# A two-layer decoder trunk: transposes in the gate's PSUM banks, a plain first gate, up before gate, and 64 bytes between tiles

## The chip, the cores and the metric

The kernel runs on one core of one Trainium2 chip. The metric is the time of one execution on the device in microseconds. An engine executes its own instructions in order and waits on semaphores for those of the others: TensorE (PE; its weight loads are listed as PEld), VectorE (DVE), ScalarE (ACT), and SyncE (SP), which issues the DMAs.

## The reference

The input is x, 256 tokens of width 2048 in float32. There are two layers, each with four attention groups behind one input projection, and a gated feed-forward part of 5632 hidden columns. What the change touches is the feed-forward part:

```
for l in range(DEPTH):                       # DEPTH = 2
    x = x + hybrid_mixer(rms_norm(x, attn_norm[l]), w_in[l], ..., w_out[l], ...)
    h = rms_norm(x, ffn_norm[l])
    x = x + (silu(h @ w_gate[l]) * (h @ w_up[l])) @ w_down[l]
return rms_norm(x, final_norm)
```

## The kernel before

x lies transposed in SBUF, in eight tiles X of 128 partitions x 2 x 256. Products are made in float32r with both factors split in a rounded part and a rest: XS holds the two parts of x times the norm's gain, and each weight becomes wh (ACT, L241) and wl (DVE, L242). A product of two split factors is three matmuls: high by high, low by high, high by low. The norm's factor itself (r_x, made by `rsq`) is applied behind the projections; `rcol` turns it by a small matmul (L424) into rxc, one number per token.

The weights come in units of 2048 columns, 1 MB each, in the order in which `pack_weights` wrote them; `fetch` gives each a raw buffer of three and one DMA on SP. wh and wl have six buffers each of 1024 columns. Three ways of multiplying matter here. `Acc.wide` and `Acc.narrow` have the weight standing still and 256 or 512 columns of x or h moving. `ProjV.step` has x standing still and 512 columns of the weight moving, 24 matmuls per unit; `up` and the v projections use it. `ProjSW.step`, the gate, does a Strassen step on blocks: seven products instead of eight, so 2 x 21 matmuls of 256 columns per unit, for which DVE builds sums of weight blocks (L348 to L353) and splits them (L354, L356), and sums of x blocks, xs_sum, are built once per layer (L762 to L777). `ProjSW.out` (L373) adds the seven products up again.

The feed-forward part runs over 11 groups of 512 hidden columns. In a group, `gate_up` takes four steps of the gate and four of `up`, in turns (in group 0 all of `up` first), makes silu(gate) times up (L796, L798), and `turn` transposes this tile `hid` with eight small matmuls (L807) and splits it into two tiles h. From group 2 on, each group is followed by four products of the down projection (`down`, eight after the last group), each of 16 pairs of a 512-column and a 256-column matmul, which `add_to` (L283, L284) adds to X. An even group turns its tile after its first down product. An odd group's tile is turned inside the next group's `gate_up`.

PSUM is divided into two tiles of two banks (accp: one for `up`, each down product and the transposes) and four of one bank (attp: the gate's seven products, and small ones). The order of the instructions on each engine is set when the program is built: the tile framework takes the program's order, lays it on a simulated timeline and issues what is ready there first. Tiles are given out pool by pool in the order of L189 to L197; the four one-line gaps of 8 floats (32 bytes) at L204 shift the pools' places within 128 bytes. In before, counted in bytes past a multiple of 128, raw lies at 0, XS, wh and wl at 32, h at 64, xs_sum at 96.

Of the kernel before, what the change touches and what calls it, by code (L numbers as in the profile page):

```python
# [8 lines left out]
F32 = mybir.dt.float32  # L9
F32R = mybir.dt.float32r  # L10
AF = mybir.ActivationFunctionType
OP = mybir.AluOpType
# [14 lines left out]
LINE = 8  # L27
RAW_B, W_B, H_B, Q_B4, T2, SG = 3, 6, 7, 8, 3, 3
NG = HID // 512

Q_LAT, KV_LAT, K_ROPE = 0, 512, 1024
Q_B, K_B, V_B = 1088, 1600, 2112
# [83 lines left out]
def pack_weights(w_in, w_uq, w_ukv, w_out, w_gate, w_up, w_down):  # L116
    us = []
    for l in range(DEPTH):
        m = w_in[l]
        us += quad_units(m, Q_LAT) + quad_units(m, KV_LAT)  # L120
        misc = np.zeros((D, 128), np.float32)
        misc[:, :64] = m[:, K_ROPE:K_ROPE + 64]
        misc[:, 64:68] = m[:, F_C:F_C + 4]
        us.append(unit(misc, 0, 16, 0, 128))

        def qkv(q0, k0, v0):
            r = []
            for c0 in (q0, q0 + 256, k0, k0 + 256):
                r += pair_units(m, c0)
            return r + quad_units(m, v0)  # L130

        us += qkv(Q_B, K_B, V_B)
        uq = w_uq[l].reshape(512, 4, 192)
        us.append(unit(uq[:, :, 128:].reshape(512, 256), 0, 4, 0, 256))
        us.append(unit(uq[:, :, :128].reshape(512, 512), 0, 4, 0, 512))
        ukv = w_ukv[l].reshape(512, 4, 256)
        us.append(unit(ukv[:, :, :128].reshape(512, 512), 0, 4, 0, 512))
        us.append(unit(ukv[:, :, 128:].reshape(512, 512), 0, 4, 0, 512))
        us += qkv(Q_C, K_C, V_C)
        us += qkv(Q_D, K_D, V_D)  # L140
        m = w_out[l]
        for c0 in range(0, D, 256):
            us.append(unit(m, 0, 6, c0, 256))
            us.append(unit(m, 6, 6, c0, 256))
        for c0 in range(0, D, 512):
            us.append(unit(m, 12, 4, c0, 512))

        def gate(g, i):
            return quarters(w_gate[l], 4 * i, 512 * g)

        def up(g, i):
            return unit(w_up[l], 4 * i, 4, 512 * g, 512)

        def dn(k0, n, ps):
            cols = 2048 // n
            return [unit(w_down[l], k0, n, c0 * cols, cols) for c0 in ps]

        for g in range(NG):
            if g == 0:
                us += [up(g, i) for i in range(4)] + [gate(g, i) for i in range(4)]  # L160
            else:
                for i in range(4):
                    us += [gate(g, i), up(g, i)]
            for c, ps in down_after(g):
                us += dn(8 * c, 8, ps)
        us += dn(8 * (NG // 2), 4, range(4))
    return np.concatenate([u.reshape(-1) for u in us])
# [17 lines left out]
def trunk(ctx: ExitStack, tc: tile.TileContext, x_d, w_d, sm_d, c_d, out_d):  # L185
# [15 lines left out]
    A.preload_act_table_set(LNEXP)  # L201

    X = [cp.tile([128, 2, S], F32, name=f"X{i}") for i in range(8)]
    for p in (cp, gp0, gp, gp1):  # L204
        p.tile([128, LINE], F32, name="gap")
    XS = [cp.tile([128, 2, 2, S], F32R, name=f"XS{i}") for i in range(8)]
    sm = cp.tile([128, SM_N], F32, name="sm")
    cst = cp.tile([128, C_N], F32, name="cst")
# [123 lines left out]

    class ProjSW:
        def __init__(self, sums):
            self.sums = sums
            ps = [attp.tile([128, 2, S], F32, name="att") for _ in range(4)]
            self.p = {1: ps[0][:, 0], 2: ps[0][:, 1], 3: ps[1][:, 0], 6: ps[2][:, 0],
                      7: ps[2][:, 1], 5: ps[3][:, 0], 4: ps[3][:, 1]}

        def step(self, k0):  # L340
            raw = fetch()
            for j in range(2):
                i = k0 // 2 + j
# [29 lines left out]
        def out(self):  # L373
            p = self.p
            c = [tp.tile([128, 512], F32, name="ff_g", tag="t2", bufs=T2) for _ in range(2)]
            c11, c12, c21, c22 = c[0][:, :256], c[0][:, 256:], c[1][:, :256], c[1][:, 256:]
            A.activation(c11, p[1], AF.Copy)
            V.tensor_add(c12, c11, p[6])
            V.tensor_add(c11, c11, p[2])
            V.tensor_add(c21, c12, p[7])  # L380
            V.tensor_sub(c12, c12, p[5])
            V.tensor_sub(c22, c21, p[5])
            V.tensor_add(c21, c21, p[4])
            V.tensor_add(c12, c12, p[3])
            return c

    def sumsq(srcs):
# [11 lines left out]
    def rsq(tot, n, name, more=None):  # L399
# [10 lines left out]
        a, ln = tot[:, 1, :], tot[:, 0, :]  # L410
        V.tensor_scalar(a, ps[:, :S], 1.0 / n, EPS, op0=OP.mult, op1=OP.add)
        A.activation(ln, a, AF.Ln)
        r0 = tp.tile([128, S], F32, name="rq_r", tag="t2", bufs=T2)
        A.activation(r0, ln, AF.Exp, scale=-0.5)
        V.tensor_mul(ln, r0, r0)
        V.scalar_tensor_tensor(a, ln, -0.5, a, op0=OP.mult, op1=OP.mult)
# [147 lines left out]
    for l in range(DEPTH):  # L564
# [190 lines left out]
        last_out(grp[3], sb + SM_FFN)  # L755
        rf = rsq(sumsq(X), D, "r_x")

        rfc = rcol(rf, "rxc")
        rfn = tp.tile([128, 2], F32, name="rfn", bufs=1)
        V.tensor_scalar(rfn, rfc, -1.0, None, op0=OP.mult)  # L760

        sums = []  # L762
        for i in range(8):
            xg = tp.tile([128, 2, S], F32, name="xg", tag="sg", bufs=SG)
# [13 lines left out]

        last_act = [None]

        def gate_up(g, turn_last):
            up = ProjV(xk, KT)
            if g == 0:
                for i in range(4):
                    up.step(4 * i)
            gate = ProjSW(sums)
            for i in range(4):
                gate.step(4 * i)
                if g > 0:
                    up.step(4 * i)  # L790
                if i == 0 and turn_last is not None:
                    turn_last()
            hid = gate.out()
            for t in range(2):
                for col, r in ((slice(0, 256), rfc), (slice(256, 512), rfn)):
                    last_act[0] = A.activation(hid[t][:, col], hid[t][:, col], AF.Silu,  # L796
                                               scale=r[:, t:t + 1])
                V.scalar_tensor_tensor(hid[t], up.out[t], rfc[:, t:t + 1], hid[t],  # L798
                                       op0=OP.mult, op1=OP.mult)
            return hid  # L800

        def turn(hid):
            pt = accp.tile([128, 2, 2, S], F32, name="acc")
            hs = [hp.tile([128, 2, 2, S], F32R, name="h") for _ in range(2)]
            for f in range(4):
                for t in range(2):
                    P.transpose(pt[:, f // 2, f % 2, t * 128:t * 128 + 128],  # L807
                                hid[t][:, f * 128:f * 128 + 128], ident)
            for p in range(2):
                split(hs[p], pt[:, p])  # L810
            hts.extend(hs)

        hts = []
# [3 lines left out]

        held = None
        for g in range(NG):
            hid = gate_up(g, None if held is None else (lambda v=held: turn(v)))  # L820
            held = hid
            if g == NG - 1:
                with tc.issue_after(last_act[0].ins):
                    A.preload_act_table_set(LNEXP)
            for n, (c, p) in enumerate((c, p) for c, ps in down_after(g) for p in ps):
                down(c, p)
                if n == 0 and g % 2 == 0:
                    turn(hid)
                    held = None
        nxt = (l + 1) * SM_L + SM_ATT if l + 1 < DEPTH else None  # L830
        last_out(lambda k: hts[4 * (NG // 2) + k // 2][:, k % 2], nxt)
# [46 lines left out]
```

## Time and profile before

| | us |
|---|---|
| median of 3 runs (2367.01 to 2367.73) | 2367.07 |
| the profiled execution, whole | 2368.98 |
| its span, first to last instruction | 2367.2 |
| PE busy in the span | 2268.4 |
| DVE busy | 1872.5 |
| ACT busy | 1271.2 |

A busy time is the time in which at least one instruction of the engine was running. Matmuls overlap, so a matmul's own duration (0.28 us for 256 columns) is not the pace at which they follow each other; the pace is read from the starts in a timeline, or from a row of the chain that merges many of them.

### The profile page before, as it was taken

The page shows a single profiled execution, that of the slowest core. Times are in us where ns is not written, and L with a number is a line of the kernel's source. Part 1 is how long each engine was busy: PE and PEld are TensorE (multiplying, and loading weights), DVE is VectorE, ACT ScalarE, POOL GpSimd, SP SyncE. Part 2 cuts the span into 40 slices and gives each one's busy share as a digit, 9 for nine tenths or more (in the row PEclk, how much of TensorE's full clock was granted, in tenths as well). Part 3 has the DMA queues.
Part 4 walks back from the last instruction along what each step waited for, and adds up shares of the span by engine and source line. Part 5 has one row for each costly group of instructions (what it writes and reads, how often), then busy time and mean ns, then how long its engine had stood idle before and what let it go on. Part 6 is the DMA issues. An engine that isn't in the chain of part 4 may idle for free.

```text
span 2367.2 us, 34828 instructions
## 1 busy us (share of the span) xinstructions
PE 2268.4 (96%) x13822; PEld 2028.1 (86%) x13822; DVE 1872.5 (79%) x2717; ACT 1271.2 (54%) x1653; POOL 0.2 (0%) x4
## 2 busy tenths in 40 slices
PE   8999999899999999999999999997999999999997
PEld 8888889688888888888998887896888888898887
DVE  7876667988887888788777765689988788797875
ACT  7454455654555545456555644656555455454554
POOL 0000000000000000000000000000000000000000
PEclk9999999999999999999999999999999999999999
DMA  7444446355554545455555344462555555454552
GB/s 290 175 155 175 141 147 212 109 179 195 196 199 177 178 177 196 163 211 196 185 189 183 129 160 143 138 218 107 196 192 182 195 196 196 161 186 170 205 205 89
DMA packets 61650, 419.90 MB, mean 177 GB/s; under 512 B 6832, under 2 KB 7088, under 8 KB 14768
## 3 DMA queue, kind: packets, MB, share of 16 engines
q1 hardware_dynamic: 61344, 417.63, 49.2%
q8 instruction: 108, 1.77, 0.3%
q14 instruction: 54, 0.44, 0.1%
q10 hardware_dynamic: 144, 0.07, 0.0%
HBM read 415.57 MB, written 2.10 MB: 176 GB/s over the span
## 4 chain that ended last, share of the span: by engine, by line
PE 90%; DVE 6%; ACT 2%; issue 1%; DMA 0%; DVEq 0%; ACTq 0%; SPq 0%
PE acc L258 67%; PE att L369 6%; PE att L370 6%; PE att L371 5%; PE att L258 4%; DVE wl L242 1%; DVE w_sum L348 1%; ACT wh L241 1%; PE acc L807 0%; PE att L492 0%; DVE w_sum L351 0%; DVE ff_g L798 0%; DVE w_sum L353 0%; PE att L501 0%; DVE wl L356 0%
## 5 line engine op out<-in xcount | busy, mean ns | idle before, releaser
L241 ACT ACTIVATE wh<-raw 128x1024 fp32r<-128x1024 f32 (+1 forms) x634 | 647.9, 1029 | 663.6 <-PE acc L258 601.9
L242 DVE TENSOR_TENSOR wl<-raw,wh 128x1024 fp32r<-128x1024 f32 (+1 forms) x634 | 744.5, 1181 | 284.2 <-ACT wh L241 282.3
L258 PE MATMUL acc<-h,wh 128*128 128x512 f32 (+1 forms) x1824 | 626.7, 389 | 32.5 <-DVE X L284 31.7
L258 PE MATMUL acc<-wh,XS 128*128 128x512 f32 x1792 | 576.4, 395 | 0.5 <-ACT wh L241 0.5
L258 PE MATMUL acc<-h,wl 128*128 128x256 f32 x1744 | 499.0, 286 | 0.0
L258 PEld LDWEIGHTS acc<-h,wh 128*128 128x128 f32 x1824 | 345.3, 192 | 103.0 <-issue 31.9
L258 PE MATMUL acc<-XS,wh 128*128 128x512 f32 (+1 forms) x1344 | 385.2, 352 | 19.6 <-DVE hilo L279 11.3
L258 PEld LDWEIGHTS acc<-wh,XS 128*128 128x128 f32 x1792 | 337.4, 188 | 75.1 <-ACT wh L241 0.7
L258 PE MATMUL acc<-wl,XS 128*128 128x512 f32 x896 | 353.6, 395 | 0.0
L258 PEld LDWEIGHTS acc<-h,wl 128*128 128x128 f32 x1744 | 337.4, 193 | 1.0
L258 PE MATMUL acc<-XS,wl 128*128 128x256 f32 x1056 | 303.0, 287 | 0.0
L258 PEld LDWEIGHTS acc<-XS,wh 128*128 128x128 f32 x1344 | 237.4, 192 | 53.2 <-DVE hilo L279 11.9
L355 ACT ACTIVATE wh<-w_sum 128x1024 fp32r<-128x1024 f32 x176 | 186.5, 1060 | 175.2 <-PE acc L258 72.3
L356 DVE TENSOR_TENSOR wl<-w_sum,wh 128x1024 fp32r<-128x1024 f32 x176 | 215.1, 1222 | 25.6 <-ACT wh L355 19.1
L354 DVE TENSOR_TENSOR wl<-raw,wh 128x768 fp32r<-128x768 f32 x176 | 167.6, 952 | 47.4 <-ACT wh L352 47.3
L258 PEld LDWEIGHTS acc<-XS,wl 128*128 128x128 f32 x1056 | 202.2, 192 | 0.8
L352 ACT ACTIVATE wh<-raw 128x768 fp32r<-128x768 f32 x176 | 148.5, 843 | 97.9 <-PE acc L258 94.8
L370 PE MATMUL att<-wh,xs_sum 128*128 128x256 f32 x704 | 197.1, 283 | 3.0 <-DVE xs_sum L776 3.0
L258 PEld LDWEIGHTS acc<-wl,XS 128*128 128x128 f32 x896 | 168.9, 188 | 35.5
L369 PE MATMUL att<-wh,xs_sum 128*128 128x256 f32 x704 | 194.6, 282 | 2.2 <-ACT xs_sum L775 1.6
L371 PE MATMUL att<-wl,xs_sum 128*128 128x256 f32 x704 | 193.9, 281 | 0.7 <-DVE wl L356 0.7
L369 PE MATMUL att<-wh,XS 128*128 128x256 f32 x528 | 150.7, 285 | 6.9 <-ACT wh L352 4.5
(187 smaller groups left out, 2758.7 us busy)
## 6 DMA issues: line engine op xcount, KB each, us to landing
raw<-in_w_dram SPq DMA_DIRECT2D x364, 1024.0 KB, 4.8
raw<-in_w_dram SPq DMA_DIRECT2D x32, 768.0 KB, 4.3
raw<-in_w_dram SPq DMA_DIRECT2D x8, 512.0 KB, 7.3
X<-in_x_dram SPq DMA_DIRECT2D x8, 256.0 KB, 6.6
out_dram<-X SPq DMA_DIRECT2D x8, 256.0 KB, 2.4
cst<-in_const_dram SPq DMA_DIRECT2D x1, 1216.0 KB, 8.7
raw<-in_w_dram SPq DMA_DIRECT2D x4, 256.0 KB, 4.8
cst<-in_const_dram SPq DMA_DIRECT2D x1, 67.0 KB, 7.4
```

Of the source, the lines that this page charges most:

```text
L241: A.activation(wh[:, i:e], raw[:, o + i:o + e], AF.Copy)
L242: V.tensor_sub(wl[:, i:e], raw[:, o + i:o + e], wh[:, i:e].bitcast(F32))
L258: P.matmul(out, lhsT, rhs, start=bank not in self.started, stop=stop, skip_group_check=True)
L348: V.tensor_add(t[:, :512].rearrange("p (a b) -> p a b", a=2), q[:, :512].rearrange("p (a b) -> p a b", a=2), q[:, 768:][:, None, :].to_bro ...
L352: A.activation(hs[:, :768], q[:, :768], AF.Copy)
L354: V.tensor_sub(ls[:, :768], q[:, :768], hs[:, :768].bitcast(F32))
L355: A.activation(ht, t, AF.Copy)
L356: V.tensor_sub(lt, t, ht.bitcast(F32))
L369: P.matmul(p, xh, wh[:, c], start=first, stop=False, skip_group_check=True)
L370: P.matmul(p, xl, wh[:, c], start=False, stop=False, skip_group_check=True)
L371: P.matmul(p, xh, wl[:, c], start=False, stop=i == 7, skip_group_check=True)
```

## The change

The transposes of `turn` take two one-bank tiles of attp, each with its own split behind it, instead of one accp tile. `ProjSW` takes its four attp tiles at its first step and not when it is made. In every group an `up` step stands ahead of the gate's step. Group 0's gate is a `ProjV` with plain weights, as wide as the Strassen one; its Silu covers 512 columns at once, and `rcol` with rxc and rfn moves behind its steps. An odd group with down products turns its tile after the last of them. In `ProjSW.out` the add of p[3] comes two operations earlier. `rsq` keeps r0 in a buffer of its own. The gap ahead of wh and wl grows from 32 to 96 bytes, which moves wh and wl to 96, h to 0 and xs_sum to 32 past a multiple of 128, while XS and raw stay.

```diff
+GAP_X, GAP_W, GAP_H, GAP_Q = 1, 3, 1, 1
...
         for g in range(NG):
-            if g == 0:
-                us += [up(g, i) for i in range(4)] + [gate(g, i) for i in range(4)]
-            else:
-                for i in range(4):
-                    us += [gate(g, i), up(g, i)]
+            for i in range(4):
+                us += [up(g, i), unit(w_gate[l], 4 * i, 4, 0, 512) if g == 0 else gate(g, i)]
...
-    for p in (cp, gp0, gp, gp1):
-        p.tile([128, LINE], F32, name="gap")
+    for p, n in ((cp, GAP_X), (gp0, GAP_W), (gp, GAP_H), (gp1, GAP_Q)):
+        p.tile([128, n * LINE], F32, name="gap")
...
             V.tensor_sub(c12, c12, p[5])
+            V.tensor_add(c12, c12, p[3])
             V.tensor_sub(c22, c21, p[5])
             V.tensor_add(c21, c21, p[4])
-            V.tensor_add(c12, c12, p[3])
...
-        r0 = tp.tile([128, S], F32, name="rq_r", tag="t2", bufs=T2)
+        r0 = tp.tile([128, S], F32, name="rq_r", bufs=1)
...
-        rfc = rcol(rf, "rxc")
-        rfn = tp.tile([128, 2], F32, name="rfn", bufs=1)
-        V.tensor_scalar(rfn, rfc, -1.0, None, op0=OP.mult)
...
         def gate_up(g, turn_last):
             up = ProjV(xk, KT)
-            if g == 0:
-                for i in range(4):
-                    up.step(4 * i)
-            gate = ProjSW(sums)
+            gate = ProjV(xk, KT) if g == 0 else ProjSW(sums)
             for i in range(4):
-                gate.step(4 * i)
-                if g > 0:
-                    up.step(4 * i)
+                up.step(4 * i)
                 if i == 0 and turn_last is not None:
                     turn_last()
-            hid = gate.out()
+                gate.step(4 * i)
+            if g == 0:
+                rc.append(rcol(rf, "rxc"))
+                rc.append(tp.tile([128, 2], F32, name="rfn", bufs=1))
+                V.tensor_scalar(rc[1], rc[0], -1.0, None, op0=OP.mult)
+                hid = [tp.tile([128, 512], F32, name="ff_g", tag="t2", bufs=T2) for _ in range(2)]
+            else:
+                hid = gate.out()
             for t in range(2):
-                for col, r in ((slice(0, 256), rfc), (slice(256, 512), rfn)):
-                    last_act[0] = A.activation(hid[t][:, col], hid[t][:, col], AF.Silu,
-                                               scale=r[:, t:t + 1])
-                V.scalar_tensor_tensor(hid[t], up.out[t], rfc[:, t:t + 1], hid[t],
+                if g == 0:
+                    A.activation(hid[t], gate.out[t], AF.Silu, scale=rc[0][:, t:t + 1])
+                else:
+                    for h in range(2):
+                        o = hid[t][:, h * 256:h * 256 + 256]
+                        last_act[0] = A.activation(o, o, AF.Silu, scale=rc[h][:, t:t + 1])
+                V.scalar_tensor_tensor(hid[t], up.out[t], rc[0][:, t:t + 1], hid[t],
                                        op0=OP.mult, op1=OP.mult)
...
         def turn(hid):
-            pt = accp.tile([128, 2, 2, S], F32, name="acc")
             hs = [hp.tile([128, 2, 2, S], F32R, name="h") for _ in range(2)]
-            for f in range(4):
-                for t in range(2):
-                    P.transpose(pt[:, f // 2, f % 2, t * 128:t * 128 + 128],
-                                hid[t][:, f * 128:f * 128 + 128], ident)
             for p in range(2):
-                split(hs[p], pt[:, p])
+                pt = attp.tile([128, 2, S], F32, name="att")
+                for f in range(2):
+                    for t in range(2):
+                        P.transpose(pt[:, f, t * 128:t * 128 + 128],
+                                    hid[t][:, (2 * p + f) * 128:(2 * p + f + 1) * 128], ident)
+                split(hs[p], pt)
...
-            hid = gate_up(g, None if held is None else (lambda v=held: turn(v)))
-            held = hid
+            hid = gate_up(g, held)
+            held = lambda v=hid: turn(v)
...
-            for n, (c, p) in enumerate((c, p) for c, ps in down_after(g) for p in ps):
+            todo = [(c, p) for c, ps in down_after(g) for p in ps]
+            for n, (c, p) in enumerate(todo):
                 down(c, p)
-                if n == 0 and g % 2 == 0:
-                    turn(hid)
+                if n == (0 if g % 2 == 0 else len(todo) - 1):
+                    held()
                     held = None
```

## Rows read from the trace of the kernel before

**Rows 1.** The page: busy time of PE, share of the span, instructions.
```profile
PE 2268.4 (96%) x13822; PEld 2028.1 (86%) x13822; DVE 1872.5 (79%) x2717; ACT 1271.2 (54%) x1653; POOL 0.2 (0%) x4
```
**Rows 2.** The waits of PE: us in total, times, longest.
```profile
PE acc L258 <- DVE X L284: 31.7, 10, 4.2
PE att L424 <- DVE r_x L418: 12.7, 2, 7.3
```
**Rows 3.** Timeline of PE (start, us, what), transposes of group 4.
```profile
840.90 1.04 PE L807 MATMUL acc<-cst,ff_g 128*128 128x128 f32 x8
845.98 0.76 PE L258 MATMUL acc<-h,wh 128*128 128x512 f32 x1 [4.05 <-DVE X L284]
...
846.76 0.63 PE L258 MATMUL acc<-h,wh 128*128 128x512 f32 x1
...
847.40 0.63 PE L258 MATMUL acc<-h,wh 128*128 128x512 f32 x1
```
**Rows 4.** Timeline of DVE in the same stretch.
```profile
845.16 0.68 DVE L284 TENSOR_TENSOR X<-X,acc 128x512 f32<-128x512 f32 x1
```
**Rows 5.** Windows: us, busy time of each engine (instructions), granted clock, DMA.
```profile
846.00:851.00 5.00, 5.00 (x15) 4.25 (x16) 0.43 (x1) 0.00 (x0) 0.00 (x0) 0.50 0.43 180
...
841.90:978.40 136.50, 132.45 (x801) 118.21 (x800) 112.68 (x151) 69.27 (x79) 0.00 (x0) 0.97 0.52 185
```
**Rows 6.** The chain that ended last (start, us, what): two steps of `up`.
```profile
597.52 5.58 PE acc L258 x24
607.98 5.58 PE acc L258 x24
```
**Rows 7.** Timeline of PE and DVE behind the gate of group 4.
```profile
829.64 0.27 PE L371 MATMUL att<-wl,XS 128*128 128x256 f32 x1
...
836.68 1.22 DVE L242 TENSOR_TENSOR wl<-raw,wh 128x1024 fp32r<-128x1024 f32 x1 [0.91 <-ACT wh L241]
837.83 1.40 DVE L798 SCALAR_TENSOR_TENSOR ff_g<-acc,rxc,ff_g 128x512 f32<-128x512 f32 x2
```
**Rows 8.** Timeline of PE: first `up` and first down matmuls of both layers.
```profile
412.53 0.40 PE L258 MATMUL acc<-wh,XS 128*128 128x512 f32 x1
...
562.94 0.28 PE L258 MATMUL acc<-h,wl 128*128 128x256 f32 x1
...
1588.52 0.40 PE L258 MATMUL acc<-wh,XS 128*128 128x512 f32 x1
...
1737.36 0.40 PE L258 MATMUL acc<-h,wh 128*128 128x512 f32 x1
```
**Rows 9.** Timeline of ACT: the table load ahead of the first Silu.
```profile
473.66 1.28 ACT L796 ACT_TABLE_LOAD   x1
```
**Rows 10.** Timeline of PE inside a gate step: nine matmuls with xs_sum, six with XS.
```profile
866.05 0.28 PE L369 MATMUL att<-wh,xs_sum 128*128 128x256 f32 x1
...
867.08 0.28 PE L369 MATMUL att<-wh,XS 128*128 128x256 f32 x1
...
867.42 0.28 PE L369 MATMUL att<-wh,XS 128*128 128x256 f32 x1
...
868.13 0.28 PE L369 MATMUL att<-wh,xs_sum 128*128 128x256 f32 x1
```
**Rows 11.** Timeline of PE in an attention projection: first and last of eleven pairs.
```profile
92.06 0.40 PE L258 MATMUL acc<-XS,wh 128*128 128x512 f32 x1
...
95.92 0.40 PE L258 MATMUL acc<-XS,wh 128*128 128x512 f32 x1
```
**Rows 12.** Groups of instructions by form: count, busy us, mean ns, idle time before.
```profile
L258 PE MATMUL acc<-wh,XS 128*128 128x512 f32 x1792 | 576.4, 395 | 0.5 <-ACT wh L241 0.5
L258 PE MATMUL acc<-wl,XS 128*128 128x512 f32 x896 | 353.6, 395 | 0.0
...
L258 PE MATMUL acc<-XS,wh 128*128 128x512 f32 x768 | 279.3, 402 | 13.6 <-DVE hilo L279 11.3 <-DVE lf L644 2.3
```
**Rows 13.** The chain again: the hidden tile of group 2, layer 0.
```profile
567.95 1.32 DVE ff_g L798 x2
```

More of the change, by code (lines that the diff above doesn't have):

```diff
@@ L334, in __init__, with banks @@
         def __init__(self, sums):
-            self.sums = sums
+            self.sums, self.p = sums, None
+        def banks(self):
             ps = [attp.tile([128, 2, S], F32, name="att") for _ in range(4)]
@@ L340, in step @@
         def step(self, k0):
+            if self.p is None:
+                self.banks()
             raw = fetch()
@@ L779, in trunk @@
         last_act = [None]
+        rc = []
         def gate_up(g, turn_last):
             up = ProjV(xk, KT)
-            if g == 0:
-                for i in range(4):
-                    up.step(4 * i)
-            gate = ProjSW(sums)
+            gate = ProjV(xk, KT) if g == 0 else ProjSW(sums)
             for i in range(4):
-                gate.step(4 * i)
-                if g > 0:
-                    up.step(4 * i)
+                up.step(4 * i)
                 if i == 0 and turn_last is not None:
                     turn_last()
-            hid = gate.out()
-            for t in range(2):
-                for col, r in ((slice(0, 256), rfc), (slice(256, 512), rfn)):
-                    last_act[0] = A.activation(hid[t][:, col], hid[t][:, col], AF.Silu,
-                                               scale=r[:, t:t + 1])
-                V.scalar_tensor_tensor(hid[t], up.out[t], rfc[:, t:t + 1], hid[t],
+                gate.step(4 * i)
[6 more added lines that the diff above has]
+                hid = gate.out()
+            for t in range(2):
+                if g == 0:
[5 more added lines that the diff above has]
+                V.scalar_tensor_tensor(hid[t], up.out[t], rc[0][:, t:t + 1], hid[t],
                                        op0=OP.mult, op1=OP.mult)
```

## The prediction

> **What bounds the kernel now.** I read the page first: TensorE (PE) is busy for 96% of the span [rows 1], so time comes only from two places, the stretches in which PE stands still and the pace at which its matmuls follow each other. The waits of PE say where it stands still [rows 2]: 31.7 us in ten waits for the vector engine's (DVE's) add into X at L284, and 12.7 us in two waits for r_x. Other idle time belongs to the attention stage, which the change does not touch. The timeline of PE then shows one of the ten: the transposes of `turn` begin at 840.90, and the next matmul of the down projection at 845.98 [rows 3]. The add that it waits for starts at 845.16, though the product it adds was finished at about 841.1 [rows 4]: two banks of accp are held by the down product and the transposes, and the add stands on DVE behind weight splits. After such a wait the granted clock is 0.50 for 5 us, the 1.2 GHz level, where the mean of the whole period is 0.97 [rows 5]: a pair of down matmuls (512 and 256 columns) then takes 0.64 us (846.76 to 847.40) [rows 3].
>
> **Part A, the transposes move to the gate's banks: takes away 48 us.** The transposes no longer take an accp bank, so the second down product finds the bank of `up` free and doesn't wait for L284; the third needs the first one's bank, but comes a whole product later, over 5.5 us, against the 4 us that the add was late. I count all 31.7 us [rows 2]. The clock's part: 55 pairs of down matmuls in all, five or eight after each of the eight long waits, run at 0.64 us [rows 3] instead of 0.35, worth 55 x 0.29 = 16 us. No DMA moves: SP's queue fetches one unit each in the new order, and `pack_weights` lays them out in that order. Bounds: all 48 us, or only the 31.7 if other waits keep the clock low.
>
> **Part B, `up` ahead of `gate`: costs 26 us.** This is the wait that the change adds. In before, after the gate's last matmul (829.64) come an `up` step (5.58 us [rows 6]) and a down product before the transposes, and the hidden tile is ready at 837.83 + 1.40 = 839.23 [rows 7]: 9.6 us, hidden under 11. With `up` first, only one down product (16 pairs x 0.35 = 5.5 us) stands behind the gate's last matmul. Then PE meets the transposes (even groups) or the second down product, which needs the bank of `up` that L798 still reads (odd groups); PE is in order, so all its later matmuls queue behind it, and the third down product with them. The same holds for groups 1 and 2, where the cover is the next group's first `up` step, also about 5.5 us. So ten groups a layer, 20 in all, can be exposed. From above: the chain stays 9.6 us long, 4.1 us uncovered each. From below: nothing, if it fits in 5.5. I take the value between by counting what lies in the chain: five weight splits at 1.14 to 1.22 us stand among its operations on DVE, one of them at 836.68 [rows 7]; without them some 3.9 us are left. In the new order only the gate's own buffers come free at that point, so I expect two or three splits there, 3.9 + 2.5 x 1.17 = 6.8 us, 1.3 us uncovered, 20 x 1.3 = 26 us. For waits this short I count no fall of the clock; its bound is the 2.3 us (8 pairs) that each long wait pays now. The moved add of p[3] lets the second half's Silu start one operation earlier; I count it at nothing.
>
> **Part C, the start of the feed-forward stage: takes away 29 us.** From the first `up` matmul to the first of the down products only, layer 0 takes 412.53 to 562.94 = 150.4 us and layer 1 takes 1588.52 to 1737.36 = 148.8 us [rows 8]. The work in it is 12 steps of gate and `up`, each 10.46 us in the steady part (597.52 to 607.98) [rows 6], and two turns of 0.9: 127.3. So 22.9 and 21.5 us are lost there, 44.4 in all. One part is the wait for r_x, 12.7 us [rows 2]: the small transposing matmul of `rcol` (L424) stands ahead of the gate on PE. The rest is DVE, which has to build weight sums and x sums at once and feeds the gate of group 0 too slowly. The change puts `rcol` behind group 0's gate, where r_x is long ready, and gives that gate plain weights, so DVE has 44 us of cheap work in which the x sums fit. What is left: plain instead of Strassen costs 24 matmuls in 5.58 us against 10.46 - 5.58 = 4.88 us per step [rows 6], 4 x 0.7 = 2.8 us a layer. Both accp banks are then held by group 0 until its Silu and product are done, with a table load of 1.28 us [rows 9] in that chain; I take 3 us a layer, and 2 us for DVE being late in groups 1 and 2. That leaves 44.4 - 2 x 7.8 = 29 us. Bounds: 39 us if only the plain matmuls cost, 10 us if DVE's lag just moves to group 1. The queue of ACT changes only by two Silus of 512 columns instead of four of 256; rq_r's own buffer can only remove a wait, and I count nothing for it.
>
> **Part D, the place of the weights: takes away 47 us.** With 64 more bytes in front of wh and wl, every tile behind them moves too. By the pools' order XS lies 32 bytes past a multiple of 128, and wh and wl do now as well: difference 0. After the change wh and wl lie at 96, difference 64. h (64, then 0) keeps its 32 to the weights, xs_sum (96, then 32) its 64. The trace of before holds both differences in one loop: in the gate, nine matmuls with xs_sum (difference 64) take 866.05 to 867.08, 0.114 us each; six with XS (difference 0) take 867.42 to 868.13, 0.118 us each [rows 10]. At the half clock a pair of 768 columns takes 0.64 us [rows 3], so its columns alone are 0.32 at the full clock, 0.107 and 0.213; a matmul at difference 64 adds 0.007 to its columns. For 512 columns I take the same: 0.220, an estimate from [rows 3, 10], against 5.58/24 = 0.2325 now [rows 6]: 0.012 less. For the attention's pairs with XS: 92.06 to 95.92 are eleven pairs, 0.351 each [rows 11], against 0.334: 0.017 less. Counts [rows 12]: 1792 + 896 = 2688 of the first kind, 768 of the second; of the 2688, 576 belong to the attention's v projections. Attention: 576 x 0.012 + 768 x 0.017 = 20 us; the narrow ones with XS I leave out. Feed-forward: (2112 + 192) x 0.012 = 28 us, and the gate 160 blocks x 12 matmuls with XS x 0.004 = 8 us. In the feed-forward stage DVE is already busy for 112.68 of 136.50 us [rows 5] and PE gets shorter by ten of them, so I take three quarters of its 36 us. 20 + 27 = 47. Bounds: 56, and nothing.
>
> The difference of 0.004 us between the two kinds in the gate is what a rule of the Trainium skill speaks against. SBUF — State Buffer, section "SBUF: two separate sides", says that TensorE's reads never wait on anyone there, and that contention comes only from a shared port; TensorE: Matmul & The Clock Gate, Part 2, gives the two operands a read port each. By that the place would change nothing and the sum would end at rival 1's time; the trace's two paces in one loop, at one shape and one clock, do not agree with it.
>
> **The sum** goes against the profiled execution: it took 2368.98 us, 2367.2 of them its span, and the median of the runs is 2367.07. Span and median stand for each other here, and the 1.8 us around the span change with nothing: 2367 - 48 + 26 - 29 - 47 = 2269.
>
> **The rivals.** *1. The place does nothing* (the change doesn't do what it says): the slower matmuls with XS would then come from the order of operands, not from the address. For it: three of the twelve xs_sum matmuls of a block, those right behind XS, are slow as well. Against it: XS is slow with whatever stands beside it. Time 2269 + 47 = 2316. *2. The hidden tile's chain takes the place of the old wait, and the kernel is slower*: DVE and ACT are in order and put weight splits into it. In group 2 of layer 0, where DVE is late, L798 ends at 569.27 [rows 13], 12 us behind the gate's last matmul. Then 6.5 us are uncovered per group, and the clock falls after each (2.3 us): 20 x 8.8 = 176 in place of 26, 2419. It decides from 9.4 us per chain on, where the wait (3.9) and the clock (2.3) cost 20 x 6.2 = 124 and all gains are gone; at the 9.6 us of before it is 2371. For it: these very splits are there. Against: the buffers that feed them come free later. *3. DVE becomes the bound in the whole feed-forward stage*: part C at its low end and the feed-forward part of D gone, 2269 + 19 + 27 = 2315.
>
> **How the numbers follow.** My forecast, from 2240 to 2297, 0.60; rival 1 or 3, to 2325, 0.23; a chain of 8 to 9.2 us, to 2362, 0.07; within 0.2% of before 0.03; rival 2 slower, 0.05; quicker than 2240, 0.02. The range 2240 to 2325 holds the first two, its low end with all of D and half of B. About 0.2% is what a measurement of this kernel can tell from no change: faster 0.92, same 0.03, slower 0.05.
>
> **What would show it.** A right: no wait of PE for L284 and no granted clock of 0.50 after the turns. B: PE's wait at L798 or behind the first down product, about 1.3 us in each group; over 4 us, rival 2. C: no wait for r_x, and the first down product some 15 us sooner after the first `up`. D: 24 `up` matmuls in 5.3 us instead of 5.58, and pairs with XS in 0.334; if they stay, rival 1. I would be wrong as a whole if L798 became PE's largest wait.

## The result, and the profile after

The changed kernel takes 2341.47 us, median of 4 runs (2336.34 to 2348.41), against 2367.14: a ratio of 0.989, 95% interval 0.987 to 0.992. It is faster, by 26 us (1.1%) and not by 98, and the time lies 16 us above the upper end of the range. The profiled execution took 2340.65 us, 2338.8 of them its span.

The waits of PE (us in total, times, longest), to be held against [rows 2]:

```profile
PE acc L256 <- DVE X L282: 52.1, 18, 3.2
PE acc L256 <- ACT ff_g L798: 8.4, 2, 4.2
```

The ten waits for the add into X have become 18 (the add is now L281 and L282), and their sum has grown from 31.7 to 52.1 us. The wait for r_x is gone; a wait for the Silu of group 0 stands in its place. One of the 18, in PE's timeline behind the gate of group 4 in layer 0 (start, us, what, idle time before and what ended it), where before has [rows 3]. (Counted from the first group as 0, the stretch of [rows 3 to 5, 7] is group 6 and not, as they are headed, group 4; group 4 waited in the same way, 136 us earlier.)

```profile
684.52 0.28 PE L256 MATMUL acc<-h,wl 128*128 128x256 f32 x1
687.83 0.47 PE L256 MATMUL acc<-h,wh 128*128 128x512 f32 x1 [3.04 <-DVE X L282]
...
691.40 1.03 PE L813 MATMUL att<-cst,ff_g 128*128 128x128 f32 x8
```

The first down product ends, the second waits, and only behind five eighths of the second do the transposes come. DVE in the same stretch (the gate's last matmul starts at 678.97), where before has [rows 4, 7]:

```profile
679.36 1.22 DVE L240 TENSOR_TENSOR wl<-raw,wh 128x1024 fp32r<-128x1024 f32 x1
...
681.16 1.22 DVE L240 TENSOR_TENSOR wl<-raw,wh 128x1024 fp32r<-128x1024 f32 x1
...
683.08 1.23 DVE L240 TENSOR_TENSOR wl<-raw,wh 128x1024 fp32r<-128x1024 f32 x1
...
684.89 0.68 DVE L281 TENSOR_TENSOR X<-X,acc 128x512 f32<-128x512 f32 x1
685.87 1.23 DVE L240 TENSOR_TENSOR wl<-raw,wh 128x1024 fp32r<-128x1024 f32 x1 [0.30 <-ACT wh L239]
687.01 0.68 DVE L282 TENSOR_TENSOR X<-X,acc 128x512 f32<-128x512 f32 x1
687.61 1.40 DVE L803 SCALAR_TENSOR_TENSOR ff_g<-acc,rxc,ff_g 128x512 f32<-128x512 f32 x2
```

Four weight splits and the add pair stand inside the chain to `hid`. L803 frees the bank of `up` at 689.01, 10.0 us behind the start of the gate's last matmul (9.6 in before [rows 7]); the first down product's bank comes free a little sooner, with L282 at 687.69, and that is what PE gets. The windows of two such places (busy time of PE, PEld, DVE, ACT, POOL, granted clock, DMA share, GB/s), for [rows 5]:

```profile
688.00:692.00 4.00, 4.00 (x26) 3.58 (x26) 3.62 (x9) 1.06 (x1) 0.00 (x0) 1.00 0.79 266
...
962.00:966.00 4.00, 4.00 (x15) 3.42 (x14) 2.38 (x6) 0.01 (x1) 0.00 (x0) 0.50 0.52 221
```

After a wait of some 3 us (3.04 here, 3.23 at 960.66) the clock stays at 2.4 GHz in one place and is at 1.2 GHz in the other. Ten of the 18 waits are followed by matmuls at the half clock, three in layer 0 and seven in layer 1.

PE's timeline at the first `up` and the first down matmul of both layers, for [rows 8], and between them the wait for group 0's Silu:

```profile
403.32 0.39 PE L256 MATMUL acc<-wh,XS 128*128 128x512 f32 x1
...
448.32 0.50 PE L426 MATMUL att<-cst,r_x 128*128 128x1 f32 x4
453.01 0.80 PE L256 MATMUL acc<-wh,XS 128*128 128x512 f32 x1 [4.18 <-ACT ff_g L798]
...
541.24 0.40 PE L256 MATMUL acc<-h,wh 128*128 128x512 f32 x1
...
1557.32 0.39 PE L256 MATMUL acc<-wh,XS 128*128 128x512 f32 x1
...
1695.06 0.40 PE L256 MATMUL acc<-h,wh 128*128 128x512 f32 x1
```

And a step of `up` in the chain that ended last, for [rows 6]; it is no shorter than it was:

```profile
487.45 5.59 PE acc L256 x24
```

From such starts each layer can be cut in three: the attention up to the first `up` matmul, the start from there to the first matmul of a down product, and the rest up to the layer's last, narrow products (22.2 us in every kernel). In layer 0 of before a few matmuls of the first down product run ahead of an `up` step, at 560.2; the cut is there, not at the 562.94 of [rows 8]. The table has the kernels that the argument needs, layer 0 / layer 1, in us; those below the second line are told of in the next section.

| kernel | attention | start | rest |
|---|---|---|---|
| before | 412.5 / 411.8 | 147.6 / 148.8 | 594.4 / 591.4 |
| after | 403.3 / 395.9 | 137.9 / 137.7 | 598.0 / 605.4 |
| e3, before with the plain gate | 412.9 / 411.9 | 128.5 / 128.5 | 592.9 / 594.8 |
| e14, before with one `up` step first | 411.8 / 413.0 | 144.8 / 146.7 | 577.8 / 576.5 |
| e9, after, transposes in accp | 404.2 / 395.8 | 130.9 / 130.4 | 613.9 / 618.9 |
| e4, after, chain covered | 404.2 / 396.5 | 139.4 / 139.0 | 565.7 / 565.7 |
| e10, e4 with transposes in accp | 404.3 / 395.6 | 128.3 / 128.4 | 574.6 / 576.3 |
| e13, the last kernel here | 403.1 / 396.4 | 131.0 / 131.0 | 561.8 / 561.8 |

After minus before: attention -9.2 and -15.9 (foreseen as untouched, apart from the place), start -9.7 and -11.1, rest +3.6 and +14.0. Together -28.3, the difference of the spans.

### The profile page after: what moved, and what is told of

Same layout as the page of the kernel before. It is cut to its first block, busy times and chain, and to the rows that moved or that the text cites. A ratio compares the mean times of both kernels' runs of the same rounds, so it can differ in the third digit from the quotient of the medians.

```text
span 2338.8 us, 34343 instructions
## 1 busy us (share of the span) xinstructions
PE 2256.6 (96%) x13678; PEld 2007.8 (86%) x13678; DVE 1834.7 (78%) x2639; ACT 1256.3 (54%) x1629; POOL 0.2 (0%) x4
## 4 chain that ended last, share of the span: by engine, by line
PE 93%; DVE 3%; ACT 2%; DMA 1%; issue 0%; ACTq 0%; DVEq 0%; SPq 0%
PE acc L256 70%; PE att L373 5%; PE att L371 5%; PE att L372 5%; PE att L256 4%; DVE wl L240 1%; ACT wh L239 1%; PE att L813 1%; DMA raw<-in_w_dram 1%; PE att L494 1%; DVE X L282 0%; PE att L484 0%; PE att L495 0%; PE att L503 0%; DMA X<-in_x_dram 0%
## 5 line engine op out<-in xcount | busy, mean ns | idle before, releaser
L239 ACT ACTIVATE wh<-raw 128x1024 fp32r<-128x1024 f32 (+1 forms) x650 | 663.6, 1027 | 744.2 <-PE acc L256 600.9
L240 DVE TENSOR_TENSOR wl<-raw,wh 128x1024 fp32r<-128x1024 f32 (+1 forms) x650 | 764.8, 1183 | 317.8 <-ACT wh L239 312.2
L256 PE MATMUL acc<-h,wh 128*128 128x512 f32 (+1 forms) x1824 | 629.1, 390 | 52.1 <-DVE X L282 52.1
L256 PE MATMUL acc<-wh,XS 128*128 128x512 f32 x1920 | 620.9, 397 | 8.4 <-ACT ff_g L798 8.4
L256 PEld LDWEIGHTS acc<-wh,XS 128*128 128x128 f32 x1920 | 362.5, 189 | 92.1 <-ACT ff_g L798 8.5
L256 PE MATMUL acc<-wl,XS 128*128 128x512 f32 x960 | 381.1, 397 | 1.0 <-DVE wl L240 1.0
L357 ACT ACTIVATE wh<-w_sum 128x1024 fp32r<-128x1024 f32 x160 | 169.8, 1061 | 143.3 <-PE acc L256 70.0
L358 DVE TENSOR_TENSOR wl<-w_sum,wh 128x1024 fp32r<-128x1024 f32 x160 | 195.7, 1223 | 38.6 <-ACT wh L357 29.9
L371 PE MATMUL att<-wh,xs_sum 128*128 128x256 f32 x640 | 178.5, 279 | 0.0
L373 PE MATMUL att<-wl,xs_sum 128*128 128x256 f32 x640 | 178.5, 279 | 0.0
L372 PE MATMUL att<-wh,xs_sum 128*128 128x256 f32 x640 | 178.5, 279 | 0.0
L371 PE MATMUL att<-wh,XS 128*128 128x256 f32 x480 | 134.6, 280 | 0.0
```

The lines of the kernel that those rows point to most:

```text
L239: A.activation(wh[:, i:e], raw[:, o + i:o + e], AF.Copy)
L240: V.tensor_sub(wl[:, i:e], raw[:, o + i:o + e], wh[:, i:e].bitcast(F32))
L256: P.matmul(out, lhsT, rhs, start=bank not in self.started, stop=stop, skip_group_check=True)
L357: A.activation(ht, t, AF.Copy)
L358: V.tensor_sub(lt, t, ht.bitcast(F32))
L371: P.matmul(p, xh, wh[:, c], start=first, stop=False, skip_group_check=True)
```

## The experiments

Each time is a median, each ratio goes against the kernel before on the same chip (2367.07 to 2368.76 us), with its 95% interval.

### Before, and one part of the change

**e1, the gap alone.**

```diff
-    for p in (cp, gp0, gp, gp1):
-        p.tile([128, LINE], F32, name="gap")
+    for p, n in ((cp, 1), (gp0, 3), (gp, 1), (gp1, 1)):
+        p.tile([128, n * LINE], F32, name="gap")
```

> The kernel before with only the gap ahead of wh and wl raised from 32 to 96 bytes (wh and wl at 96, h at 0, xs_sum at 32; XS stays at 32). The step of the prediction: 0.012 us less for each of 2688 matmuls of 512 columns with XS and 0.017 less for each of 768 attention pairs, so 2320 us (47 less). Rival, the place does nothing in sum: within 5 us of before, 2362 to 2368, with 24 up matmuls still in 5.5 to 5.6 us.

2360.99 us, ratio 0.996 (0.995 to 0.998). Eight us, not 47, near what rival 1 said of the time. But the place does act, where the prediction had read it. The same stretch of a gate step as in [rows 10], in PE's timeline of e1: nine matmuls with xs_sum, nine with XS.

```profile
865.95 0.28 PE L369 MATMUL att<-wh,xs_sum 128*128 128x256 f32 x1
...
866.97 0.28 PE L369 MATMUL att<-wh,XS 128*128 128x256 f32 x1
...
867.99 0.28 PE L369 MATMUL att<-wh,xs_sum 128*128 128x256 f32 x1
```

Both kinds take 0.113 us now. Those with XS have lost the 0.004 us by which they were slower, with nothing changed but addresses. By the mean paces in the table of places further down, some 6 us of the gain come from the matmuls with XS and some 4 from those with xs_sum; the 512-column ones take 2 back.

**e2, the buffer of rq_r alone.**

```diff
-        r0 = tp.tile([128, S], F32, name="rq_r", tag="t2", bufs=T2)
+        r0 = tp.tile([128, S], F32, name="rq_r", bufs=1)
```

> The kernel before with only a buffer of its own for r0 in rsq. The changed kernel spends 9.2 us less ahead of the first up matmul of layer 0 and 15.9 us less in the attention of layer 1, which the prediction counted at nothing. If that is the shared buffer (rsq waiting for a t2 tile, and all of the attention's order with it): 25 us less, 2342 us, and the waits of PE for hilo at L279 (11.3 us) gone. Rival, the attention's gain comes from the weights' new place: within 3 us of before, 2364 to 2370.

2344.13 us, ratio 0.990 (0.988 to 0.991): 25 us from the part that the prediction had counted at nothing. In before, DVE stands at L415 waiting for rq_r, and the add L279, which has to empty an accp bank, is queued behind it (DVE's timeline of before):

```profile
1443.02 0.42 DVE L415 TENSOR_TENSOR sq<-rq_r 128x256 f32<-128x256 f32 x1 [2.23 <-ACT rq_r L414]
1443.51 0.69 DVE L279 TENSOR_TENSOR hilo<-acc,lo 128x512 f32<-128x512 f32 x1
```

PE waits 5.6 us for that L279, and 11.3 in three such places. With the buffer, the program that is laid down has L279 ahead (DVE of e2):

```profile
1422.44 0.69 DVE L279 TENSOR_TENSOR hilo<-acc,lo 128x512 f32<-128x512 f32 x1
1425.25 0.43 DVE L415 TENSOR_TENSOR sq<-rq_r 128x256 f32<-128x256 f32 x1 [2.12 <-ACT rq_r L414]
```

The waits for L279 are gone from its list. They are 11.3 of the 25 us; 4 us of other waits of PE in the two attention stages go with them, and by the starts some 6 us of matmuls below their full pace.

**e3, the plain gate of group 0 alone** (`rcol` behind it).

```diff
             if g == 0:
+                gate = ProjV(xk, KT)
                 for i in range(4):
                     up.step(4 * i)
+                    gate.step(4 * i)
+                rc.append(rcol(rf, "rxc"))
...
```

> The kernel before with only group 0 changed: plain gate, up and gate in turns, rcol behind it. The prediction's part C: 15 us less per layer between the first up and the first down matmul, 2338 us in all, with the wait for r_x (12.7 us) gone. In the changed kernel the same stretch is 9.7 and 11.1 us shorter, with about 2.3 us of clock and 4.4 us of waiting behind group 0 in it: by that 2346 us. Rival, the lag of the vector engine only moves into group 1: 5 us or less, above 2360.

2332.89 us, ratio 0.985 (0.984 to 0.987): 36 us, all of it in the start (table). Part C is real, and larger than it was put.

**e8, the transposes in attp alone.**

```diff
-            pt = accp.tile([128, 2, 2, S], F32, name="acc")
...
             for p in range(2):
+                pt = attp.tile([128, 2, S], F32, name="att")
```

> The kernel before with the transposes alone changed: two one-bank tiles of attp in place of one two-bank tile of accp, each with its own split behind it; order, first gate, gaps and buffers as before. Prediction's part A: the waits for L284 (31.7 us) and the half clock behind them (16 us) go: 2367 - 48 = 2319 us. Rival: only the idle time goes, the clock's part does not: 2335 us. Second rival: the transposes now wait for the gate's banks, or the next gate for theirs, and the wait only changes its place: 2355 to 2370 us.

2387.01 us, ratio 1.009 (1.007 to 1.010): slower by 20 us. Its second rival had the mechanism, but no reading had the size. An odd group's transposes belong behind the next group's first gate step; there the gate holds all four banks of attp, so they come only after its last step, and the down products that need their h wait (PE of e8, behind the gate of group 4):

```profile
699.92 0.60 PE L808 MATMUL att<-cst,ff_g 128*128 128x128 f32 x4
...
706.42 0.51 PE L258 MATMUL acc<-h,wh 128*128 128x512 f32 x1 [1.93 <-DVE h L440]
```

In before the same transposes ran at 667.08, in the middle of that gate. With no transposes in accp any more, six waits for L284 are still in its list, 18.0 us in all.

**e14, the first `up` step ahead alone** (the transposes stay in accp; those of an odd group now come ahead of the next gate's first step and not behind it).

```diff
-                for i in range(4):
+                us += [up(g, 0), gate(g, 0)]
+                for i in range(1, 4):
                     us += [gate(g, i), up(g, i)]
...
+            else:
+                up.step(0)
+                if turn_last is not None:
+                    turn_last()
...
-                if g > 0:
+                if g > 0 and i > 0:
```

> The kernel before with only the first up step of groups 1 to 10 moved ahead of the first gate step (order up, gate, gate, up, gate, up, gate, up); transposes in accp, Strassen gate in group 0, buffers and gap as before. Theory: the ten waits for L284 (31.7 us, with 16 us of half clock behind them) come from VectorE, which at that point builds the weight sums of the next group's first gate step (L348 to L353, 2.9 us) ahead of the add; with an up step next it has only splits to do there, the waits fall to under 10 us in all and the time is 2367 - 36 = 2331 us. Rival: they come from the two accp banks, as the prediction's part A had it; then the ten waits stay at 4 us and the time is 2360 us or more.

2331.77 us, ratio 0.985 (0.984 to 0.987). The ten waits for L284 fall from 31.7 to 11.9 us in all, though the banks are those of before. What stood ahead of the add in before were, beside two weight splits, sums for the next group's first gate step (DVE of before, behind the gate of group 4):

```profile
703.33 1.29 DVE L348 TENSOR_TENSOR w_sum<-raw 128x512 f32<-128x512 f32 x2
...
705.68 0.75 DVE L351 TENSOR_TENSOR w_sum<-w_sum,raw 128x256 f32<-128x256 f32 x2
706.35 0.68 DVE L283 TENSOR_TENSOR X<-X,acc 128x512 f32<-128x512 f32 x1
...
709.35 0.68 DVE L284 TENSOR_TENSOR X<-X,acc 128x512 f32<-128x512 f32 x1
```

With an `up` step next they come behind it (DVE, then PE of e14):

```profile
697.15 0.69 DVE L284 TENSOR_TENSOR X<-X,acc 128x512 f32<-128x512 f32 x1 [0.21 <-PE acc L259]
697.87 0.69 DVE L285 TENSOR_TENSOR X<-X,acc 128x512 f32<-128x512 f32 x1
698.48 1.22 DVE L243 TENSOR_TENSOR wl<-raw,wh 128x1024 fp32r<-128x1024 f32 x1
699.61 1.29 DVE L349 TENSOR_TENSOR w_sum<-raw 128x512 f32<-128x512 f32 x2
...
698.70 0.47 PE L259 MATMUL acc<-h,wh 128*128 128x512 f32 x1 [0.72 <-DVE X L285]
```

PE waits 0.7 us there, where it waited 4.2.

### After, and one part undone or covered

**e4, the chain covered**: from group 1 on the order is up, gate, gate, up, gate, up, gate, up.

```diff
+def gu_order(g):
+    r = []
+    for i in range(4):
+        r += [("up", i), ("gate", i)] if g == 0 or i == 0 else [("gate", i), ("up", i)]
+    return r
```

> The changed kernel with one thing undone: from group 1 on, each group still begins with an up step, but then the gate's step comes ahead of up's, so that the group ends with an up step of 5.5 us as it did before. Theory: the 18 waits for L282 (52.1 us) and the slow clock behind some of them (53 pairs x 0.29 = 16 us) come from the hidden tile's chain of about 10 us, which keeps up's bank while only one down product of 5.5 us covers it. Then all of it goes: 2273 us, and granted clock above 0.995. Rival, the add of L282 is late because the vector engine's queue is full of weight splits, whatever the order: 30 us or more of waits for it stay, 2320 us or more.

2270.69 us, ratio 0.959 (0.958 to 0.961), 71 us under after. An `up` step now stands between the gate's last matmul and the first down product. No wait for the add into X is left in its list, and all of the gain is in the rest (table).

**e7, the bank of `up` freed early**, after's order kept.

```diff
+                if i == 3 and g > 0:
+                    for t in range(2):
+                        upc.append(tp.tile([128, 512], F32, name="up_c", tag="sg", bufs=SG))
+                        A.activation(upc[t], up.out[t], AF.Copy, scale=rc[0][:, t:t + 1])
                 gate.step(4 * i)
...
+                    V.tensor_mul(hid[t], upc[t], hid[t])
```

> The changed kernel, its order kept (up ahead of gate in each group), but ACT copies the up product with the norm's factor out of PSUM as soon as the fourth up step is done, so that its accp bank is free long before the gate's sums and Silu are. Theory: the 18 waits of 3.2 us for L282 come from the second down product taking the first one's bank because up's bank is still held; then they go, with the half clock behind them, and the time is 2341 - 52 - 16 = 2273 us, up to 2285 with the two 1.1 us copies per group on ACT. Rival: DVE and ACT are late with the add itself and the chain to the transposes has no cover in any case; then most of the waits stay and the time is 2320 us or more.

2264.16 us, ratio 0.956 (0.955 to 0.958), a little under the 2273 to 2285 of its theory. The add is no earlier than it was, and nobody waits for it: the second down product starts in the bank that the copies freed. ACT and DVE of e7 behind the same group, whose gate's last matmul starts at 672.54:

```profile
668.09 1.26 ACT L791 ACTIVATE up_c<-acc,rxc 128x512 f32<-128x512 f32 x2 [1.69 <-PE acc L256]
...
681.81 0.68 DVE L282 TENSOR_TENSOR X<-X,acc 128x512 f32<-128x512 f32 x1
682.41 0.69 DVE L811 TENSOR_TENSOR ff_g<-up_c,ff_g 128x512 f32<-128x512 f32 x1
```

So in the changed kernel the held bank makes the wait, and the chain's lateness matters only through it.

**e9, after with the transposes back in accp; e10, e4 with them back.** Both have the same edit:

```diff
+            pt = accp.tile([128, 2, 2, S], F32, name="acc")
...
-                pt = attp.tile([128, 2, S], F32, name="att")
```

> The changed kernel with the transposes back in one two-bank tile of accp; all else as changed. If part A's 48 us are in the changed kernel and only covered up by part B: 2341 + 48 = 2389 us. Rival: since in the changed order the second down product waits for the first one's bank anyway, the transposes' bank is only one more claim on the same two and costs 10 to 20 us: 2351 to 2361 us. Second rival: nothing, 2341 us.

> The kernel with an up step at the end of each group (order up, gate, gate, up, gate, up, gate, up from group 1 on; 2270.69 us) with the transposes back in one two-bank tile of accp. Prediction's part A, a mechanism of its own once the chain is covered: the waits for the add into X and the half clock come back, 2271 + 48 = 2319 us, with 6 or more waits of some 4 us for the add. Rival: part A is worth little, the order of the rest decided in the kernel before too: under 2290 us.

e9: 2358.78 us, ratio 0.996 (0.995 to 0.998), 17 us over after, the first rival. e10: 2269.84 us, ratio 0.959 (0.957 to 0.960), the same as e4. The zero is a difference of two things (table): attp is better by 9 to 11 us a layer in the rest and worse by 11 in the start, where the transposes of group 0 and the first Strassen gate want the same four banks.

**e11, `up` copied in group 0 too (edit against e7), and e13, with the transposes of groups 0 and 1 in accp besides (edit against e11).**

```diff
-                if i == 3 and g > 0:
+                if i == 3:
...
+            if g < 2:
+                pt = accp.tile([128, 2, 2, S], F32, name="acc")
```

> The changed kernel with up copied out of PSUM by ACT as soon as it is whole in every group, group 0 too (without the norm's factor there, which comes with the product as before). From 2264.16 us with the copies from group 1 on: the two waits of 4.2 us for group 0's Silu, the 0.9 us behind them and some ten matmuls at half clock go, 2264 - 12 = 2252 us. Rival: up of group 1 then waits for the same chain through the gate's own bank of accp, which group 0's Silu still reads: 2260 us or more.

> The kernel with up copied out of PSUM in every group (2262.47 us), with the transposes of groups 0 and 1 in one two-bank tile of accp and those of all later groups in attp. Theory: in the start of the stage, where the transposes of group 0 and the first gate with sums both want attp's four banks and no down product claims accp, accp is the better place, as in the run with all transposes in accp (128.3 instead of 139.4 us a layer): 2262 - 21 = 2241 us. Rival: the order of up ahead of gate keeps TensorE waiting for group 0's Silu all the same: 2255 us or more.

e11: 2262.47 us, ratio 0.956 (0.954 to 0.957), level with e7: the wait for group 0's Silu stays at 8.4 us, as its rival said. e13: 2247.6 us, ratio 0.949 (0.948 to 0.951), between its theory (2241) and its rival (2255 or more). PE goes from `rcol` straight into the gate of group 1, where after waits until 453.01:

```profile
448.08 0.50 PE L426 MATMUL att<-cst,r_x 128*128 128x1 f32 x4
448.44 0.36 PE L371 MATMUL att<-wh,XS 128*128 128x256 f32 x1
```

It is the fastest kernel here, 94 us under after, and its start is 131.0 us, 2.7 over that of e10.

### The place, three times more

**e5, e6, e12**: after, e4 and e11 with the gap back at 32 bytes.

```diff
-GAP_X, GAP_W, GAP_H, GAP_Q = 1, 3, 1, 1
+GAP_X, GAP_W, GAP_H, GAP_Q = 1, 1, 1, 1
```

> The changed kernel with the gap ahead of the weights put back to 32 bytes; all else as changed. Prediction's part D (the place takes away 47 us): 2341 + 47 = 2388 us. Rival 1 (the place does little; alone on the kernel before it took 8 us): 2341 to 2352 us, and the gate's matmuls back at 0.118 to 0.121 us each where the changed kernel has 0.113 to 0.118.

> The changed kernel with the steps of each group from group 1 on in the order up, gate, gate, up, gate, up, gate, up (2270.69 us with the 96-byte gap) and the gap back at 32 bytes. If the place takes time off wherever PE is the bound, PE now being busy for 99%, it costs more here than in the kernel before: 2270.7 + 20 = 2291 us or more. If it takes what it took alone on the kernel before, 8 us: 2279 us. If nothing: 2271 us.

> The kernel with up copied in every group, with the gap ahead of the weights at 32 bytes instead of 96. By the paces of the runs so far (256-column matmuls 115.8 to 117.2 ns with 96 bytes and 117.3 with 32; 512-column ones 231.7 and 231.05): some 7600 x up to 1.5 ns more and 5290 x 0.65 ns less, 0 to 8 us slower than with 96 bytes. Prediction's part D would be 47 us slower.

e5: 2330.76 us (0.983 to 0.986), e6: 2269.89 us (0.957 to 0.960), e12: 2271.78 us (0.958 to 0.961). So 96 bytes instead of 32 are worth -8 us in before (e1), +11 in after, +1 in e4 and -9 in e11. The mean distance of matmul starts in ns, with waits and half-clock stretches left out:

| | gate, with XS | gate, with xs_sum | `up` and v, 512 columns |
|---|---|---|---|
| 32 bytes: before, e5, e6, e12 | 118.1, 118.0, 117.7, 118.0 | 115.6, 115.3, 115.2, 115.5 | 232.3, 232.4, 232.4, 232.5 |
| 96 bytes: e1, after, e4, e11 | 114.3, 116.1, 117.0, 114.2 | 113.8, 115.9, 116.8, 113.7 | 233.1, 233.2, 233.2, 233.1 |

With 96 bytes the difference between XS and xs_sum is gone in every kernel, and the 512-column matmuls are 0.8 ns slower in every one. The means differ because in after and e4 whole gate steps run at 118 ns a matmul, with either operand: of 74 undivided steps of after, 30 take 113 to 114 ns and 44 take 117.5 to 118, whole groups at the one or the other, for the most part in turns. In e1 all 50 take 113 to 114, in before all 50 take 115.5 to 116.5. What sets a group to 118 no run here shows. The +11 in after (9 between the profiled executions) goes with the clock: ten of its 18 waits are followed by the half clock, in e5 three of 18 at nearly the same length, at 1.3 to 3.0 us each. By the starts, matmuls that are below their full pace without a wait cost 43 us in after and 32 in e5. In the four runs of after the mean clock went from 0.990 in the quickest to 0.984 in the slowest; whether the place makes falls more frequent no run here shows.

## Why the prediction was wrong

**The sum.** Forecast 2367 - 48 (A) + 26 (B) - 29 (C) - 47 (D) = 2269. By the runs: -36 for C (e3), -25 for rq_r (e2), -36 for the first `up` step ahead (e14) and -8 for the place (e1) make 2262, where e4 and e10, which have all these, take 2270; the transposes' place adds nothing there (e10 against e4); the last three `up` steps ahead of the gate add 71 (after against e4): 2341. The moved add of p[3] and the later turn of odd groups were not tried alone, nor were the gate's banks taken at its first step. They lie in the 8 us between 2262 and 2270, together with what the parts do to each other (in e4 the place is worth +1 and not -8). The measured time falls into the stretch that the prediction gave 0.07, "a chain of 8 to 9.2 us, to 2362"; that is luck, since the chain took 10.0 us and the other terms were off both ways.

**Part A failed at its cause.** The prediction saw in [rows 4] that the add stood behind other work on DVE, and yet gave all 48 us to the banks. e14 shows the queue: the same banks, another step next, and 36 us are gone. The bank change alone is worth +20, -17 or 0, by the order around it (e8, e9, e10). In the changed kernel the step that fails is "the second down product finds the bank of `up` free": L803 reads that bank until 689.01, as the prediction itself says in part B for odd groups. "No wait of PE for L284" was the test, and it failed with 52.1 us for the same add, now L282.

**Part B had the right mechanism, and was mis-sized.** The second down product does stop for the bank of `up`, in groups 2 to 10 of both layers, even or odd; behind group 1 only some 0.7 us are lost, at 504. The chain to `hid` was put at 6.8 us with "two or three splits". That step failed: the chain takes 10.0 us, where before took 9.6, with four splits and the add pair in it. (Before has four splits there too, and not the five that the prediction counted.) The splits are those of the weights for the products that follow; the trace of after has them where that of before has them [rows 7]. So 3.04 us are uncovered in most groups instead of 1.3, within the 0 to 4.1 of the bounds, 52 us in all. The rest of the 71 is the clock, which the prediction let stay up: by the starts, matmuls slower than full pace without a wait cost 43 us in after and 27 in e4, 16 of the 19 us that remain. Rival 2 was near on the chain (9.4 us as its point) but not on the outcome: it counted 6.2 us a group with the clock, and 3.5 came out (71 over 20 groups), since the wait ends with the first product's bank, ahead of the chain, and the clock falls after ten of the 18 waits only.

**Part C was right in kind and sign.** Alone it gives 36 us, in the bounds of 10 to 39; in the changed kernel the start is shorter by only 9.7 + 11.1 = 21. The 3 us counted for group 0's Silu are a wait of 4.2 (4.4 between starts) with ten matmuls at the half clock behind it, some 2 us more, and 0.7 us at 504; e9 and e10 show that this loss, 7 us a layer in after and 11 in e4, hangs on the transposes' place, a part that was costed on its own. Two readings of the sum were off without weight in it: 150.4 less 127.3 is 23.1 and not 22.9, and layer 0's first down matmul is at 560.15, which makes it 20.3.

**Part D failed at one estimate, the largest.** The gate's part held in kind: XS lost its 0.004 us with the place alone (e1). The 8 us counted for it are about what e1 gained, but partly by luck: a block has nine matmuls with XS, not twelve, which makes 6, and the rest came from xs_sum. So rival 1 was near on what the place is worth (nothing, where 8 us came) and wrong in its reason, the order of operands. What failed is the step "for 512 columns I take the same: 0.220", made from two paces of 256-column matmuls [rows 10]: these matmuls went from 232.3 to 233.1 ns, `up` takes 5.59 us where 5.3 was to be seen, the attention's pairs with XS stay at 0.352 us where 0.334 was, and with it fell the attention's 20 us and the 28 in the feed-forward part. The rule of the Trainium skill that stood against the rows (SBUF — State Buffer, "SBUF: two separate sides": TensorE's reads don't wait there) would have given the better sum; the pace of the XS matmuls in e1 does not agree with it, by 3.8 ns in 118.

**The part left out.** "Other idle time belongs to the attention stage, which the change does not touch" was wrong. The wait for L279 has a row in the list of groups [rows 12] (11.3 us of idle time), and a buffer of its own for rq_r is an edit in that stage. It "can only remove a wait", and what it removed was worth 25 us.

## What to carry to other kernels

When a matmul waits for an add, first ask what stands ahead of the add on its engine, and which later step put that there; only then whether another buffer would help. An order of steps has two ends: putting cheap work first freed DVE for the adds (36 us), and leaving none of it at the end uncovered a chain (71 us), so one step moved was better than four. Where the order has to stay, a copy that frees the bank ahead of the chain does the same (77 us, e7). Parts that use the same banks can't be costed one by one: the same edit was worth +20, -17 and 0.

## What the runs showed of the hardware

After waits of the same 3.04 us the granted clock was at 1.00 in one place (1913.2 in after) and at 0.50 in the next (1981.0). It was at 0.50 behind ten of 18 such waits in one kernel and behind three of 18 in one that differs by 64 bytes. The runs of the changed kernel spread by 12 us, those of e4, which has no such wait, by under 3. In the changed kernel the gate's 256-column matmuls ran at two steady paces, 113 and 118 ns, that changed from group to group, at the full clock and with the same operands; in e1, with the tiles at the same places within 128 bytes, there was only 113.
